# Delta rule and block inverses: small matmuls of different parts of the array written in turns, and both halves of the heads in shared tiles

## The chip, the cores and the metric

One core of a Trainium2 chip runs the whole kernel. The metric is the device time of one execution in microseconds; lower is better. Three runs of the kernel before gave a median of 1875.55 us (1871.42 to 1876.63).

## What is computed

Two layers of a decoder trunk on 1024 tokens of width 1024: an RWKV-7 mixer (16 heads of 64), then differential attention, each followed by a gated per-layer embedding, and a last norm. The change lies in the mixer's recurrence, which the reference writes token by token:

```
def step(state, inp):
    r_t, w_t, k_t, v_t, kk_t, b_t = inp
    sa = jnp.einsum('bhij,bhj->bhi', state, kk_t)
    state = (state * w_t[:, :, None, :] - sa[..., None] * b_t[:, :, None, :]
             + v_t[..., None] * k_t[:, :, None, :])
    y_t = jnp.einsum('bhij,bhj->bhi', state, r_t)
    return state, y_t
```

The kernel works in 16 chunks of 64 tokens. In a chunk the delta rule becomes the product with the inverse of a triangular 64x64 matrix for each head; the state passes from chunk to chunk.

## The kernel before

The 16 heads are two halves, `st` = 0 and 1, of eight heads each: four pairs `p_`, and in a pair the heads `h` = 0 and 1, one on partitions 0 to 63 and one on 64 to 127. A 64x64 product of one head uses 64 rows of the TensorE array (the partitions of its operands) and 64 columns (the partitions of its result). An fp32 product that is written once shows as two matmul records in the trace, each with its own weight load; I call each of them a pass. Transposes and the rounded fp32 products of the dense layers show as one.

**Stage of the inverses** (327 to 598 us). While the dense products for v (`v`, line 75 to 77) and for the gate (`d`) run on PE, four inversions of four chunks each are laid between them. `inv_pb` makes `pb` (line 512; rows of `h`, columns of `st`), which VectorE scales into `nq` (line 514); `inv_diag` inverts 32x32 blocks by 31 steps of two VectorE operations (`tm`, `tb`, lines 541 and 543); `inv_merge` joins the blocks by the products `pg` and `po` (lines 576 and 590; rows and columns of `st`), which ScalarE copies.

**Stage of the chain** (598 to 958 us). For chunk `c`:

- `chain_x`: `xy` gets state times `kkr` (line 827, all rows and columns), then adds `m` times `vu` (line 832; rows of the other half, columns of `st`). ScalarE copies it to `x` (line 842). GpSimd makes `spl`, the decayed state (line 839).
- `chain_u`: `u` is the inverse `ti` times `x` (line 851; rows and columns of `st`); VectorE scales it into the other half of `vu` (line 853).
- `chain_s`: `s` is `kbn` times `vu` (line 867; all rows, columns of `h`), which VectorE adds to `spl` as the new `state` (line 868); the output part of `xy` gets `m` times `vu` (line 871; all rows, the columns of the other half), and ScalarE copies it to `y` (line 874).

Before, each function is called for `st` = 0, then for `st` = 1. Between them `fill` lays other work: `stage1` of the next chunk (`pm`, line 175: 64 rows of `h` and all 128 columns, which VectorE masks into `m` at line 176; the transposes `kbt` at line 168 and `prt` at line 155, read by ScalarE as `kbn` and by VectorE as `bon`) and `d1_pieces` of finished chunks: group norm of `y` (`gst`, lines 904 to 921), its transposes `ytr` (line 932, read by VectorE as `sg`) and the output product `op`. `pm`, `kbt`, `prt` and `ytr` share one ring of two PSUM buffers, the tag that `ps1` holds:

```
pm = ps1[0].tile([P, 4, P], F32, tag=ps1[1], name=f"pm{h}{u}", bufs=2)
```

The order on each engine is fixed when the program is built, by a scheduler that begins with the order in which the program is written, and moves instructions by priority and readiness. At run time each engine takes its instructions in that order.

Of the kernel before, what the change touches and what calls it, by code (L numbers as in the profile page):

```python
# [21 lines left out]
P = 128  # L22
# [4 lines left out]
L = 64  # L27
# [10 lines left out]
def trunk(ctx: ExitStack, tc: tile.TileContext, A, out):  # L38
# [92 lines left out]
    def stage1(st, c):  # L131
# [39 lines left out]
        def mh(h):  # L171
            hs = slice(h * 64, h * 64 + 64)
            pm = ps1[0].tile([P, 4, P], F32, tag=ps1[1], name=f"pm{h}{u}", bufs=2)
            for p_ in range(4):
                T.matmul(pm[:, p_], lhsT=kb[hs, p_], rhs=kkr[hs, p_], start=True, stop=True)  # L175
            V.tensor_tensor(out=m[:, h], in0=pm, in1=early["mmask"][:, st:st + 1].to_broadcast([P, 4, P]), op=ALU.mult)  # L176

        return [(load, 0), (lambda: mh(0), 850), (turn, 430), (lambda: mh(1), 850), (bonus, 430)]

    with NB("ab") as ab, NP("psab") as pp:  # L180
# [313 lines left out]
        def inv_pb(q):  # L494
# [3 lines left out]
            for cc in range(4):  # L498
# [3 lines left out]
                for t, src in ((bb, kb_d), (kk, kkr_d)):  # L502
                    for st in range(2):
                        js = slice(4 * st, 4 * st + 4)
                        nc.sync.dma_start(out=t[:, js], in_=src[js, :, c, st].rearrange("j p l -> p j l"))
                for h in range(2):
                    hs_ = slice(h * 64, h * 64 + 64)
                    pb = pp.tile([P, 4, L], F32, tag="aux", name=f"pb{c}{h}", bufs=2)
                    for st in range(2):
                        o = 64 * st  # L510
                        for p_ in range(4):
                            T.matmul(pb[o:o + 64, p_], lhsT=bb[hs_, 4 * st + p_], rhs=kk[hs_, 4 * st + p_],
                                     start=True, stop=True)
                    V.tensor_tensor(out=nq[:, cc, h], in0=pb,
# [49 lines left out]
        def inv_merge(q):  # L564
# [4 lines left out]
            prhs, pairs = ivt  # L569
            for st in range(2):  # L570
                o = 64 * st
                pg = pp.tile([P, 16, 32], F32, tag="tr", name=f"pg{q}{st}", bufs=2)
                for x in range(16):
                    if x == 8:
                        yield
                    T.matmul(pg[o:o + 64, x], lhsT=pairs[o:o + 64, x], rhs=prhs[o:o + 64, x], start=True, stop=True)
                for y in range(2):
                    r, hs_ = slice(o + 32 * y, o + 32 * y + 32), slice(16 * y, 16 * y + 16)
                    S.copy(pairs[r, :, 32 * y:32 * y + 32], pg[r])
                    S.copy(prhs[r], ti[o + 32:o + 64, hs_, 32:64])  # L580
                yield
            for _ in range(Y2):
# [999 lines left out]
```

## Time and profile before

| | us |
|---|---|
| median of three runs | 1875.55 |
| the profiled execution, its own time | 1872.35 |
| its span, first to last instruction | 1870.6 |
| PE busy | 1786.7 |
| VectorE (DVE) busy | 1348.5 |
| ScalarE (ACT) busy | 762.4 |
| GpSimd (POOL) busy | 635.7 |
| stage of the inverses | 327 to 598 |
| stage of the chain | 598 to 958 |

A busy time counts an engine as busy while any of its instructions is in flight. Matmuls are pipelined, so a PE that is busy throughout can still be waiting for weight loads; what a stream of matmuls costs is read from the distance of one start to the next in the timeline.

### The profile page before, as it was taken

The page shows a single profiled execution, that of the slowest core. Times are in us where ns is not written, and L with a number is a line of the kernel's source. Part 1 is how long each engine was busy: PE and PEld are TensorE (multiplying, and loading weights), DVE is VectorE, ACT ScalarE, POOL GpSimd, SP SyncE. Part 2 cuts the span into 40 slices and gives each one's busy share as a digit, 9 for nine tenths or more (in the row PEclk, how much of TensorE's full clock was granted, in tenths as well). Part 3 has the DMA queues.
Part 4 walks back from the last instruction along what each step waited for, and adds up shares of the span by engine and source line. Part 5 has one row for each costly group of instructions (what it writes and reads, how often), then busy time and mean ns, then how long its engine had stood idle before and what let it go on. Part 6 is the DMA issues. An engine that isn't in the chain of part 4 may idle for free.

```text
span 1870.6 us, 30495 instructions
## 1 busy us (share of the span) xinstructions
PE 1786.7 (96%) x11320; PEld 1485.4 (79%) x11320; DVE 1348.5 (72%) x3083; ACT 762.4 (41%) x1594; POOL 635.7 (34%) x705
## 2 busy tenths in 40 slices
PE   6899899999999999999999999899999999999998
PEld 5677678898787888888878878788888888777786
DVE  7878945587994566666676666877887887866765
ACT  6565533246344222223243433444444444444332
POOL 4436635124224444445420044323323323221200
PEclk9999999898999999999999999999999999999999
DMA  7125344433325443334263321101101101341121
GB/s 260 41 69 161 126 113 96 113 103 102 85 66 178 154 138 102 109 112 124 87 208 113 118 94 48 43 20 52 37 26 52 33 30 52 112 138 33 57 90 68
DMA packets 164402, 175.98 MB, mean 94 GB/s; under 512 B 74845, under 2 KB 127837, under 8 KB 164254
## 3 DMA queue, kind: packets, MB, share of 16 engines
q1 hardware_dynamic: 161950, 169.84, 29.5%
q10 hardware_dynamic: 2304, 4.20, 0.6%
q8 instruction: 89, 1.46, 0.3%
q14 instruction: 59, 0.48, 0.1%
HBM read 124.19 MB, written 49.81 MB: 93 GB/s over the span
## 4 chain that ended last, share of the span: by engine, by line
PE 79%; DVE 14%; issue 2%; DMA 2%; ACT 1%; POOL 0%; SPq 0%; DVEq 0%; ACTq 0%; POOLq 0%
PE qkv L75 6%; PE qkv L76 6%; PE qkv L77 6%; PE d L75 4%; PE d L77 4%; PE d L76 4%; PE pm L175 4%; PE av L1306 3%; DVE xmt L216 2%; PE sc L1266 2%; PE xy L832 2%; PE sc L1267 2%; PE xy L827 2%; PE u L851 2%; PE fg L77 2%
## 5 line engine op out<-in xcount | busy, mean ns | idle before, releaser
L1276 ACT ACTIVATE e<-sc,mx 128x256 f32<-128x256 f32 (+7 forms) x128 | 94.1, 739 | 111.0 <-DVE mx L1273 60.0
L1220 POOL TENSOR_TENSOR rp<-rp,rq 128x128 f32<-128x128 f32 x64 | 34.8, 544 | 239.3 <-DVE rq L1215 191.4
L176 DVE TENSOR_TENSOR m<-pm,mmask 128x512 f32<-128x512 f32 x64 | 44.2, 690 | 67.2 <-PE pm L175 66.4
L1306 PE MATMUL av<-vh,aT 128*128 128x128 f32 x576 | 81.0, 280 | 6.3 <-DVE aT L1302 6.3
L1306 PEld LDWEIGHTS av<-vh,aT 128*128 128x128 f32 x576 | 75.4, 195 | 12.9 <-DVE aT L1302 9.0
L175 PE MATMUL pm<-kkr,kb 64*128 64x128 f32 x512 | 75.8, 286 | 0.0
L1272 DVE TENSOR_REDUCE mxs<-sc 128x1 f32<-128x128 f32 (+6 forms) x112 | 74.1, 681 | 0.5
L1266 PE MATMUL sc<-k,q 128*128 128x512 f32 (+2 forms) x192 | 71.5, 379 | 2.2 <-ACT e L1276 2.2
L175 PEld LDWEIGHTS pm<-kkr,kb 64*128 64x128 f32 x512 | 62.2, 187 | 12.1 <-issue 5.3
L216 DVE SCALAR_TENSOR_TENSOR xmt<-hT,cB,xmt 128x512 f32<-128x512 f32 x64 | 63.8, 1016 | 5.4 <-POOL ti L562 4.9
L164 POOL TENSOR_TENSOR kbp<-kb,plast 128x512 f32<-128x512 f32 x32 | 37.2, 1164 | 87.0 <-PE kbt L168 76.1
L1267 PE MATMUL sc<-k,q 128*128 128x512 f32 (+2 forms) x192 | 64.8, 348 | 0.0
L1308 ACT ACTIVATE o<-av,r 128x128 f32<-128x128 f32 x64 | 23.5, 368 | 90.8 <-PE av L1306 90.8
L1288 DVE SCALAR_TENSOR_TENSOR e<-e,r,e 128x128 f32<-128x128 f32 (+3 forms) x64 | 56.5, 883 | 1.2
L541 DVE TENSOR_TENSOR tm<-tb,nb 128x31 f32<-128x31 f32 (+15 forms) x124 | 53.7, 433 | 3.6
L839 POOL TENSOR_TENSOR spl<-state,plast 64x256 f32<-64x256 f32 x60 | 46.1, 769 | 29.6 <-DVE state L868 21.7
L1214 DVE TENSOR_TENSOR rp<-qkv,rc 128x256 f32<-128x256 f32 x64 | 27.0, 423 | 39.9 <-PE qkv L77 33.0
L543 DVE TENSOR_TENSOR tb<-tb,tm 128x31 f32<-128x31 f32 (+15 forms) x124 | 53.4, 430 | 3.4
L1248 POOL CAST q<-q 64x128 fp32r<-64x128 f32 x128 | 38.8, 304 | 48.8 <-PE sc L1267 44.6
L1239 POOL CAST k<-k 64x256 fp32r<-64x256 f32 x64 | 26.4, 413 | 81.2 <-ACT k L1237 80.0
L1302 DVE COPY aT<-at 128x512 f32<-128x512 f32 (+2 forms) x96 | 52.0, 550 | 1.1 <-PE at L1300 0.4
L1300 PE MATMUL at<-ident,e 128*128 128x128 f32 x288 | 47.4, 277 | 2.9 <-DVE e L1288 2.3
(1180 smaller groups left out, 6155.1 us busy)
## 6 DMA issues: line engine op xcount, KB each, us to landing
pp_d<-ppo SPq DMA_DIRECT2D x32, 256.0 KB, 2.2
kb_d<-kb SPq DMA_DIRECT2D x16, 512.0 KB, 2.6
kkr<-kkr_d SPq DMA_DIRECT2D x32, 256.0 KB, 3.0
kb<-kb_d SPq DMA_DIRECT2D x32, 256.0 KB, 2.9
x<-in_x SPq DMA_DIRECT2D x8, 512.0 KB, 5.3
kkr_d<-ep SPq DMA_DIRECT2D x16, 256.0 KB, 2.6
kkr_d<-rt SPq DMA_DIRECT2D x16, 256.0 KB, 2.6
bb<-kb_d SPq DMA_DIRECT2D x32, 128.0 KB, 2.6
```

The costliest lines, as they stand in the source:

```text
L75: T.matmul(ps, lhsT=ah, rhs=bh, start=start, stop=False)
L76: T.matmul(ps, lhsT=ah, rhs=bl, start=False, stop=False)
L77: T.matmul(ps, lhsT=al, rhs=bh, start=False, stop=stop)
L175: T.matmul(pm[:, p_], lhsT=kb[hs, p_], rhs=kkr[hs, p_], start=True, stop=True)
L216: V.scalar_tensor_tensor(out=t, in0=hT[:, kt, half(hf)], scalar=cB[:, g, kt:kt + 1], in1=t, op0=ALU.mult, op1=ALU.add)
L541: V.tensor_tensor(out=tv, in0=tb[:, j:j + 1, 0:w].to_broadcast([P, n, w]), in1=nb[:, j + 1:32, j:j + 1].to_broadcast([P, n, w]), op=ALU.mult)
L1266: T.matmul(ps[:, b0:b1], lhsT=q1[:, m, ts_], rhs=k1[:, m, b0:b1], start=True, stop=False)
L1267: T.matmul(ps[:, b0:b1], lhsT=q0[i % 2][:, m], rhs=k2[:, b0:b1], start=False, stop=True)
L1272: V.tensor_reduce(out=seed, in_=ps[:, 0:n - P], axis=AX.X, op=ALU.min)
L1276: S.activation(e[:, 0:n], ps[:, 0:n], AF.Exp, scale=-1.0, bias=mx, accum_out=l_[:, m:m + 1])
L1288: V.scalar_tensor_tensor(out=es[0][:, 0:n], in0=es[1][:, 0:n], scalar=r[:, 1:2], in1=es[0][:, 0:n], op0=ALU.mult, op1=ALU.add)
L1306: T.matmul(po, lhsT=aT[kb // 4][:, kb % 4], rhs=c["vh"][:, kb], start=(kb == 0), stop=(kb == i))
```

## The change

`turns` gives each matmul of a list an order dependency on the one before it, without a semaphore: it fixes the order on PE and adds no wait. With it

- `pm` is made for both `h` at once, the two row halves in turns, into both buffers of the ring;
- `pb` is made for both `h` and both `st` in turns (four quarters of the array);
- `pg` and `po` for both `st` in turns, and the copies follow after one more step of the tick;
- the chain's functions take both halves: `xy` (second part), `u` and the output part with `st` = 1 and 0 in turns, `s` with the two `h` in turns. Its matmuls have high priority;
- `vu` and `x` are one tile for both halves, and `vu` of the next chunk is loaded at the head of `chain_x`;
- the two transposes `ytr` of a pair of chunks are called one chunk earlier, at the end of that chunk's list (`ahead`).

No product and no VectorE, ScalarE or GpSimd operation of the mathematics is added or taken away. The core of the diff:

```diff
+    def turns(ms):
+
+        for a, b in zip(ms, ms[1:]):
+            tc.add_manual_dep(b.ins, a.ins.name,
+                              mybir.DependencyInfo(mybir.DependencyClass.NoSync, mybir.DependencyReason.DATA),
+                              reason="turns")
...
-        def mh(h):
-            hs = slice(h * 64, h * 64 + 64)
-            pm = ps1[0].tile([P, 4, P], F32, tag=ps1[1], name=f"pm{h}{u}", bufs=2)
+        def mh():
+
+            pm = [ps1[0].tile([P, 4, P], F32, tag=ps1[1], name=f"pm{h}{u}", bufs=2) for h in range(2)]
+            ms = []
             for p_ in range(4):
-                T.matmul(pm[:, p_], lhsT=kb[hs, p_], rhs=kkr[hs, p_], start=True, stop=True)
-            V.tensor_tensor(out=m[:, h], in0=pm, in1=early["mmask"][:, st:st + 1].to_broadcast([P, 4, P]), op=ALU.mult)
-
-        return [(load, 0), (lambda: mh(0), 850), (turn, 430), (lambda: mh(1), 850), (bonus, 430)]
+                for h in (1, 0):
+                    hs = slice(h * 64, h * 64 + 64)
+                    ms.append(T.matmul(pm[h][:, p_], lhsT=kb[hs, p_], rhs=kkr[hs, p_], start=True, stop=True))
+            turns(ms)
+            for h in range(2):
+                V.tensor_tensor(out=m[:, h], in0=pm[h],
+                                in1=early["mmask"][:, st:st + 1].to_broadcast([P, 4, P]), op=ALU.mult)
+
+        return [(load, 0), (turn, 430), (mh, 850), (bonus, 430)]
...
+                pb = [pp.tile([P, 4, L], F32, tag="aux", name=f"pb{c}{h}", bufs=2) for h in range(2)]
+                ms = []
+                for p_ in range(4):
+                    for st in (1, 0):
+                        o = 64 * st
+                        for h in (1, 0):
+                            hs_ = slice(h * 64, h * 64 + 64)
+                            ms.append(T.matmul(pb[h][o:o + 64, p_], lhsT=bb[hs_, 4 * st + p_],
+                                               rhs=kk[hs_, 4 * st + p_], start=True, stop=True))
+                turns(ms)
...
+            def products(nm):
+                pg = [pp.tile([P, 16, 32], F32, tag="tr", name=f"{nm}{q}{st}", bufs=2) for st in range(2)]
+                ms = []
+                for x in range(16):
+                    for st in (1, 0):
+                        r = slice(64 * st, 64 * st + 64)
+                        ms.append(T.matmul(pg[st][r, x], lhsT=pairs[r, x], rhs=prhs[r, x], start=True, stop=True))
+                turns(ms)
+                return pg
...
+        def vload(c):
+            vu = co.tile([P, 2, 4, 2, L], F32, tag="vu", name=f"vu{c}", bufs=2)
+            for st in range(2):
+                nc.sync.dma_start(out=vu[64 - 64 * st:128 - 64 * st, st].rearrange("p j h l -> p (j h l)"),
+                                  in_=v_d[c * L:(c + 1) * L, st * 512:st * 512 + 512])
+            vus[c] = vu
...
+        def chain_x(c):
+
+            px_, ms = [], []
+            vu2 = vus.pop(c)
+            if c + 1 < NCH:
+                vload(c + 1)
...
+                with tc.high_priority():
+                    ms += [T.matmul(px_[st][:, p_].rearrange("p h l -> p (h l)"), lhsT=kkr[:, p_],
+                                    rhs=state[st][:, p_], start=(p_ == 0), stop=False, skip_group_check=True)
+                           for p_ in range(4)]
+            with tc.high_priority():
+                for p_ in range(4):
+                    for h in range(2):
+                        for st in (1, 0):
+                            xs_, ys_, vu, px = ctx_c[st]
+                            m = units[st, c][2]
+                            ms.append(T.matmul(px[xs_, p_, h], lhsT=m[ys_, h, p_, half_(st)], rhs=vu[ys_, p_, h],
+                                               start=False, stop=True, skip_group_check=True))
+            turns(ms)
+            x = co.tile([P, 4, 2, L], F32, tag="x", name=f"x{c}", bufs=1)
...
+        def chain_u(c):
...
+                        for st in (1, 0):
+                            xs_, x = ctx_c[st][0], ctx_c[st][5]
+                            ms.append(T.matmul(pu[st][xs_, p_, h], lhsT=ti[xs_, (c % 4) * 8 + h * 4 + p_],
+                                               rhs=x[xs_, p_, h], start=True, stop=True))
+            turns(ms)
...
+        def chain_s(c):
...
+                        ms += [T.matmul(pS[half_(h), p_], lhsT=kbn[:, p_, half_(h)], rhs=vu[:, p_, h],
+                                        start=True, stop=True) for p_ in range(4) for h in range(2)]
...
+                        for st in (1, 0):
+                            xs_, ys_, vu, px = ctx_c[st][:4]
+                            ms.append(T.matmul(px[ys_, p_, h], lhsT=units[st, c][2][:, h, p_, half_(1 - st)],
+                                               rhs=vu[:, p_, h], start=False, stop=True, skip_group_check=True))
+            turns(ms)
...
+                    if x == 2 and c < NCH - 3:
+
+                        ahead.append((c + 2, pc[:2]))
+                        pc = pc[2:]
```

Three places of the built order show it. **PE, the transposes at the head of chunk 6** (`xy0`, `xy1` are the halves of the chain's tile, `pm01_6` is `h` 0 of half 1 of chunk 6, `ytr10` a transpose for the finished chunks 2 and 3). Before:

```order
L175 MATMUL pm11_6_6809<-kkr1_6_6630,kb1_6_6631 128x128 x4
L867 MATMUL s1_5_6781<-vu1_5_6654,kbn1_5_6405 64x64 x4
L827 MATMUL xy0_6_6853<-state0_5478,kkr0_6_6626 128x128 x4
L155 MATMUL prt1_6_6837<-ident_60,pr1_6_6834 128x128 x2
L832 MATMUL xy0_6_6853<-vu0_6_6851,m0_6_6628 64x64 x8
L175 MATMUL pm00_7_6893<-kkr0_7_6843,kb0_7_6844 128x128 x4
L827 MATMUL xy1_6_6873<-state1_5480,kkr1_6_6630 128x128 x4
L932 MATMUL ytr10_6899<-ident_60,y1_5925 128x128 x4
L832 MATMUL xy1_6_6873<-vu1_6_6871,m1_6_6632 64x64 x8
```

and now:

```order
L855 MATMUL xy1_6_6872<-state1_5480,kkr1_6_6623 128x128 x4
L185 MATMUL pm11_6_6755<-kkr1_6_6623,kb1_6_6624 128x128
L185 MATMUL pm01_6_6754<-kkr1_6_6623,kb1_6_6624 128x128
L185 MATMUL pm11_6_6755<-kkr1_6_6623,kb1_6_6624 128x128
L185 MATMUL pm01_6_6754<-kkr1_6_6623,kb1_6_6624 128x128
L185 MATMUL pm11_6_6755<-kkr1_6_6623,kb1_6_6624 128x128
L185 MATMUL pm01_6_6754<-kkr1_6_6623,kb1_6_6624 128x128
L185 MATMUL pm11_6_6755<-kkr1_6_6623,kb1_6_6624 128x128
L185 MATMUL pm01_6_6754<-kkr1_6_6623,kb1_6_6624 128x128
L981 MATMUL ytr10_6825<-ident_60,y1_5924 128x128 x4
L864 MATMUL xy1_6_6872<-vu6_6627,m1_6_6625 64x64
L864 MATMUL xy0_6_6867<-vu6_6627,m0_6_6621 64x64
```

`pm` alternates between the row halves and fills both buffers of the ring, and `ytr10`, which needs one of them, stands right behind it.

**PE, `xy` and `u` of chunk 4.** Before, one half after the other:

```order
L832 MATMUL xy0_4_6408<-vu0_4_6406,m0_4_6148 64x64 x8
L832 MATMUL xy1_4_6428<-vu1_4_6426,m1_4_6152 64x64 x8
L932 MATMUL ytr00_6454<-ident_60,y0_5488 128x128 x4
L851 MATMUL u0_4_6503<-x0_4_6424,ti1_2685 64x64 x8
L851 MATMUL u1_4_6513<-x1_4_6444,ti1_2685 64x64 x8
L932 MATMUL ytr01_6465<-ident_60,y0_5488 128x128 x4
```

and now (the piece begins with the last three of 16):

```order
L864 MATMUL xy0_4_6426<-vu4_6151,m0_4_6145 64x64
L864 MATMUL xy1_4_6431<-vu4_6151,m1_4_6149 64x64
L864 MATMUL xy0_4_6426<-vu4_6151,m0_4_6145 64x64
L162 MATMUL prt1_4_6398<-ident_60,pr1_4_6395 128x128 x2
L890 MATMUL u1_4_6505<-x4_6452,ti1_2685 64x64
L981 MATMUL ytr01_6403<-ident_60,y0_5487 128x128 x4
L890 MATMUL u0_4_6504<-x4_6452,ti1_2685 64x64
L890 MATMUL u1_4_6505<-x4_6452,ti1_2685 64x64
L890 MATMUL u0_4_6504<-x4_6452,ti1_2685 64x64
L890 MATMUL u1_4_6505<-x4_6452,ti1_2685 64x64
```

Consecutive matmuls now lie in different rows and columns of the array, and both halves of `u` begin only when both halves of `x` are copied.

**VectorE, between the states of chunk 5 and the first `sg` of chunk 6** (`m1_6` are the evictions of `pm11_6` and `pm01_6` above; `gst2` and `y2` the group norm of chunks 4 and 5). Before:

```order
L868 TENSOR_TENSOR state0_5478<-s0_5_6761,spl0_5_6649 64x4x64
L176 TENSOR_TENSOR m1_6_6632<-pm01_6_6745,mmask_5234 128x512
L868 TENSOR_TENSOR state1_5480<-s1_5_6781,spl1_5_6669 64x4x64
L868 TENSOR_TENSOR state0_5478<-s0_5_6761,spl0_5_6649 64x4x64
L904 TENSOR_REDUCE gst2_7057<-y2_6397 128x16
L176 TENSOR_TENSOR m1_6_6632<-pm11_6_6809,mmask_5234 128x512
L868 TENSOR_TENSOR state1_5480<-s1_5_6781,spl1_5_6669 64x4x64
L905 TENSOR_SCALAR gst2_7057<-gst2_7057 128x16
L159 TENSOR_REDUCE bon_76<-prt1_6_6837 64x2x2 x2
L906 TENSOR_TENSOR y2_6397<-y2_6397,gst2_7057 128x1024
L176 TENSOR_TENSOR m0_7_6845<-pm00_7_6893,mmask_5234 128x512
L935 SCALAR_TENSOR_TENSOR sg1_6608<-ytr10_6899,vecs_65,sg1_6608 128x128 x4
```

and now:

```order
L910 TENSOR_TENSOR state0_5478<-s0_5_6785,spl0_5_6657 64x4x64 x2
L910 TENSOR_TENSOR state1_5480<-s1_5_6796,spl1_5_6661 64x4x64 x2
L166 TENSOR_REDUCE bon_76<-prt0_6_6729 64x2x2 x2
L953 TENSOR_REDUCE gst2_7046<-y2_6414 128x16
L954 TENSOR_SCALAR gst2_7046<-gst2_7046 128x16
L955 TENSOR_TENSOR y2_6414<-y2_6414,gst2_7046 128x1024
L963 TENSOR_REDUCE gst2_7046<-ysq2_7050 128x16
L188 TENSOR_TENSOR m1_6_6625<-pm11_6_6755,mmask_5234 128x512
L188 TENSOR_TENSOR m1_6_6625<-pm01_6_6754,mmask_5234 128x512
L68 TENSOR_SCALAR gst2_7046<-gst2_7046 128x16
L984 SCALAR_TENSOR_TENSOR sg1_6601<-ytr10_6825,vecs_65,sg1_6601 128x128 x4
```

The states of both halves are updated together, and both evictions of `pm` now stand behind two reductions (`gst2`) and a subtraction (`y2`) of the group norm, where before one stood between the states and the other behind one reduction.

## Rows read from the trace of the kernel before

**Rows 1.** The page: busy times with shares, and the chain's shares by engine.

```profile
PE 1786.7 (96%) x11320; PEld 1485.4 (79%) x11320; DVE 1348.5 (72%) x3083; ACT 762.4 (41%) x1594; POOL 635.7 (34%) x705
PE 79%; DVE 14%; issue 2%; DMA 2%; ACT 1%; POOL 0%; SPq 0%; DVEq 0%; ACTq 0%; POOLq 0%
```

**Rows 2.** Windows by stage: us, busy by engine (count), PE clock, DMA share, GB/s.

```profile
327.00:598.00 271.00, 260.33 (x2128) 226.18 (x2126) 207.19 (x367) 116.81 (x190) 74.12 (x56) 0.93 0.36 101
598.00:958.00 360.00, 358.56 (x3388) 302.36 (x3389) 228.95 (x447) 96.99 (x150) 168.41 (x167) 0.99 0.41 124
```

**Rows 3.** Waits of PE in the chain's stage: total us, times, longest.

```profile
PE xy L832 <- DMA vu<-v_d: 1.3, 1, 1.3
```

**Rows 4.** Timeline of PE in chunk 8: start us, length us, what, count.

```profile
783.13 1.06 PE L827 MATMUL xy<-state,kkr 128*128 128x128 f32 x8
784.12 1.16 PE L175 MATMUL pm<-kkr,kb 64*128 64x128 f32 x8
785.20 1.90 PE L832 MATMUL xy<-vu,m 64*64 64x64 f32 x32
787.03 1.09 PE L932 MATMUL ytr<-ident,y 128*128 128x128 f32 x8
788.05 1.90 PE L851 MATMUL u<-x,ti 64*64 64x64 f32 x32
```

**Rows 5.** The same timeline, 8 us later: two column halves meet.

```profile
793.14 0.27 PE L871 MATMUL xy<-vu,m 128*64 128x64 f32 x1
793.19 0.22 PE L867 MATMUL s<-vu,kbn 128*64 128x64 f32 x1
793.24 0.22 PE L871 MATMUL xy<-vu,m 128*64 128x64 f32 x1
793.25 0.22 PE L867 MATMUL s<-vu,kbn 128*64 128x64 f32 x1
793.30 0.22 PE L871 MATMUL xy<-vu,m 128*64 128x64 f32 x1
```

**Rows 6.** Windows of chunk 7 and chunk 8, columns as in rows 2.

```profile
762.20:781.90 19.70, 19.70 (x205) 16.52 (x203) 7.94 (x14) 4.64 (x8) 7.89 (x11) 1.00 0.40 128
781.90:806.00 24.10, 24.10 (x226) 20.61 (x226) 19.94 (x45) 5.63 (x9) 13.41 (x13) 1.00 0.33 95
```

**Rows 7.** Groups of VectorE in these chunks: busy us, mean ns, idle before.

```profile
L176 DVE TENSOR_TENSOR m<-pm,mmask 128x512 f32<-128x512 f32 x8 | 5.5, 690 | 9.1 <-PE pm L175 9.0
L868 DVE TENSOR_TENSOR state<-s,spl 64x256 f32<-64x256 f32 x8 | 3.4, 422 | 4.0 <-PE s L867 3.6 <-issue 0.3
L159 DVE TENSOR_REDUCE bon<-prt 64x4 f32<-64x256 f32 x8 | 3.4, 421 | 0.2
L853 DVE TENSOR_TENSOR vu<-u,rn 64x512 f32<-64x512 f32 x4 | 2.7, 685 | 0.9 <-PE u L851 0.9
L904 DVE TENSOR_REDUCE gst<-y 128x16 f32<-128x1024 f32 x1 | 1.2, 1221 | 0.0
L914 DVE TENSOR_REDUCE gst<-ysq 128x16 f32<-128x1024 f32 x1 | 1.2, 1220 | 0.5 <-ACT ysq L908 0.5
```

**Rows 8.** Groups of ScalarE in these chunks.

```profile
L842 ACT COPY x<-xy 64x512 f32<-64x512 f32 x4 | 2.3, 580 | 6.7 <-PE xy L832 6.7
L908 ACT ACTIVATE ysq<-y 128x1024 f32<-128x1024 f32 x1 | 1.1, 1057 | 4.7 <-DVE y L906 4.7
```

**Rows 9.** Timeline of PE in the inverses' stage: products of both kinds.

```profile
450.73 0.96 PE L512 MATMUL pb<-kk,bb 64*64 64x64 f32 x16
...
541.15 3.71 PE L590 MATMUL po<-prhs,pairs 64*64 64x32 f32 x64
```

**Rows 10.** Windows in the inverses' stage, and chunk 4 (687.0 to 714.8).

```profile
350.00:575.00 225.00, 222.95 (x1839) 193.56 (x1838) 191.47 (x343) 101.90 (x166) 64.28 (x44) 0.95 0.34 95
475.00:550.00 75.00, 75.00 (x528) 59.35 (x528) 71.34 (x138) 33.40 (x52) 19.96 (x13) 0.98 0.22 68
687.00:714.80 27.80, 26.46 (x221) 22.56 (x221) 22.24 (x45) 8.84 (x13) 9.56 (x13) 0.88 0.34 97
```

More of the change, by code (lines that the diff above doesn't have):

```diff
@@ L505, in inv_pb @@
                         nc.sync.dma_start(out=t[:, js], in_=src[js, :, c, st].rearrange("j p l -> p j l"))
-                for h in range(2):
[L507 to L514, printed above, removed]
+                pb = [pp.tile([P, 4, L], F32, tag="aux", name=f"pb{c}{h}", bufs=2) for h in range(2)]
[8 more added lines that the diff above has]
+                turns(ms)
+                for h in range(2):
+                    V.tensor_tensor(out=nq[:, cc, h], in0=pb[h],
                                     in1=rn[:, c, h].unsqueeze(2).to_broadcast([P, 4, L]), op=ALU.mult)
@@ new lines, in chain_u @@
+        def chain_u(c):
+            ti = tis[c // 4]
+            pu = [pp.tile([P, 4, 2, L], F32, tag="us", name=f"u{st}_{c}", bufs=2) for st in range(2)]
+            ms = []
+            with tc.high_priority():
+                for p_ in range(4):
+                    for h in range(2):
+                        for st in (1, 0):
[3 more added lines that the diff above has]
+            turns(ms)
+            for st in range(2):
+                xs_, vu = ctx_c[st][0], ctx_c[st][2]
+                V.tensor_tensor(out=vu[xs_], in0=pu[st][xs_],
+                                in1=rn[xs_, c].rearrange("p h j -> p j h").unsqueeze(3).to_broadcast([64, 4, 2, L]),
+                                op=ALU.mult)
@@ new lines, in chain_s @@
+        def chain_s(c):
+            ms = []
+            if c < NCH - 1:
+                for st in range(2):
+                    vu, spl, kbn = ctx_c[st][2], ctx_c[st][4], units[st, c][1]
+                    pS = pp.tile([P, 4, L], F32, tag="us", name=f"s{st}_{c}", bufs=2)
+                    with tc.high_priority():
+                        ms += [T.matmul(pS[half_(h), p_], lhsT=kbn[:, p_, half_(h)], rhs=vu[:, p_, h],
+                                        start=True, stop=True) for p_ in range(4) for h in range(2)]
+                    for h in range(2):
+                        hs = half_(h)
+                        V.tensor_tensor(out=state[st][hs, :, hs], in0=pS[hs], in1=spl[hs], op=ALU.add)
+            with tc.high_priority():
+                for p_ in range(4):
+                    for h in range(2):
+                        for st in (1, 0):
[3 more added lines that the diff above has]
+            turns(ms)
@@ L974, in weave @@
             return o
-        for st in range(2):
-            vus[st] = vload(st, 0)
+        vload(0)
         later = [[] for _ in range(NCH + 6)]
@@ L1004, in early_row @@
             return lambda: wg.append(gate_row(0, q, None, EG[q], er[0][:, q], False))
+        ahead = []
         EG = (G, G)
@@ L1011, in trunk @@
                 D1[c // 2] = {"y": dt_("y", f"y{c // 2}", 3)}
+            for at_, pc in ahead:
+                if at_ == c:
+                    later[c].extend(pc)
             work = weave(stage1(0, c + 1) + stage1(1, c + 1) if c + 1 < NCH else [], later[c])
```

108 lines of the change are left out of this document (32 added, 76 removed).

## The prediction, made before the changed kernel ran

> **What bounds the kernel now.** I read the page first: PE is busy 96% of the span, and 79% of the chain that ended last runs on it [rows 1]. The windows by stage say where the change can act: in the chain's stage (598 to 958 us) PE is busy for 358.56 of 360 us and VectorE for 228.95, in the inverses' stage for 260.33 of 271 and 207.19 [rows 2]. In the chain PE waits for another engine in a way that matters only once, 1.3 us for the load of `vu` [rows 3]. So PE's own stream sets the time of the chain, and what is saved there is saved, until something else is late.
>
> What a pass costs is read from starts in the timeline of chunk 8. 32 passes of `xy` take 1.83 us from 785.20 to the next group at 787.03, 57 ns each; 32 of `u` look the same; eight of `pm` take 1.08 us (784.12 to 785.20), 135 ns each, the change of tile shape included [rows 4]. These neighbours use the same part of the array. Eight microseconds later, where the program happens to pass from `s` to the output part of `xy`, passes of the two column halves start two by two: 793.14, 793.19, 793.24, 793.25, 793.30 [rows 5]. Each half keeps its own distance of 53 to 58 ns and both run at once. This is what `turns` makes the rule.
>
> **A rule against it.** Both groups of rows 5 use all 128 rows, on different columns, and run side by side [rows 5]. The Trainium skill (TensorE: Matmul & The Clock Gate, Part 3: Packing small matmuls) says that a weight load overlaps matmuls in flight only when the row group differs. The trace disagrees for column halves. By the rule `s` and the output part would gain nothing, and the sum would be 1819.
>
> **The chain, part by part**, for chunks 7 and 8, which take 19.70 and 24.10 us, 43.8 together [rows 6]:
>
> - `pm`: eight groups of eight passes, 8 x 1.08 = 8.7 us. Now four groups of 16, eight on each row half; if the halves run side by side a group takes what eight take now, 1.08 us: 4.3 us less. No row shows two row halves over the same columns side by side. The ends are nothing (they run one after the other) and the full 4.3; a loss is excluded, as the same passes remain and their groups get fewer. I take the full gain, since the nearest row, two column halves, shows no cost of company [rows 5].
> - `xy` (second part) and `u`: 1.83 us each and chunk [rows 4]. Now 16 passes on each half, at 57 ns, and some 0.15 us for the change of tile shape (an estimate: at the 53 ns of rows 5, 32 passes would take 1.70 of the 1.83): 1.07 us. Less 0.76 four times: 3.0 us.
> - `s` and the output part: 64 passes a chunk in halves, 32 x 0.057 + 0.15 = 2.0 us. In chunk 8 they now take about 3.1, as some already run in pairs [rows 5]: less 1.1 twice, 2.2 us.
>
> Together 9.5 us of PE per two chunks, 43.8 to 34.3; eight times 76 us. The first part of `xy` fills the array and stays.
>
> **What is late next.** Until now one half's matmuls covered ScalarE and VectorE of the other. Now both halves hand over together, and three waits appear, as I read the built order.
>
> First, `ytr10` stands right behind `pm` of the next chunk, which fills both buffers of the ring. It must wait for the first eviction `m`, and on VectorE that stands behind four state updates (1.7 us), two `bon` (0.8), a reduction (1.2), a subtraction of the same size (1.2), ScalarE's square (1.06), the next reduction (1.2), and takes 0.7 [rows 7, 8]: 7.8 us, with hand-offs and one small operation 8.4 after the end of `s`. PE comes there earlier: output part 1.1, `prt` and `kbt` 0.9 (six transposes; eight take 1.02), first part of `xy` 2.0 (twice the 0.99 from 783.13 to 784.12), `pm` 1.1, in all 5.1 [rows 4]. So PE stands some 3.3 us in every second chunk. Behind it on PE wait the second part of `xy`, so `x`, `u` and the chain.
>
> Second, `u` waits for two copies to `x`, 2 x 0.58 [rows 8], and `s` for two scalings, 2 x 0.69 [rows 7]. About two thirds of these lie under `kbt` and `pm`, which stand between; I leave 1.0 us per two chunks, more where no dense product stands there.
>
> VectorE as a whole has 27.9 us of work in these two chunks [rows 6], below the new 34.3 + 4.3 = 38.6, so it does not become the bound over two chunks, only inside the heavy one. GpSimd's 21.3 is further away [rows 6].
>
> Waits: 4.3 us for each of six pairs of chunks, 1 us for the first two, which have no transposes to wait for: 28 us. Against it, the load of `vu` a chunk ahead takes away the wait of rows 3 and the lower granted clock behind it: chunk 4 takes 27.80 us at a mean clock of 0.88, chunk 8 with the same work 24.10 at 1.00 [rows 6, 10]: 3 us. The two loads per chunk stay two on SP's queue, issued earlier; their buffer is free one chunk before. `turns` itself carries no semaphore and costs nothing; if the fixed order makes a ready matmul stand behind one that is not, that is within the waits. The chain: 76 + 3 - 28 = 51 us less.
>
> **The inverses.** `pg` and `po` are eight groups of 64 passes, 3.6 us each [rows 9]; two halves side by side halve them: 8 x 1.75 = 14 us. `pb` is 32 groups of 16 passes, 0.96 us with its tail [rows 9], about 1 us with the change of shape, now 16 groups of 32 at two abreast, about 1.1: 32 x 1.0 less 16 x 1.1, 14 us. I assume two and not four abreast for the four quarters, as no row shows more. Together 28 us on PE, 30 with the group changes. But VectorE is close there: 191.5 us busy of 225 between 350 and 575, and 71.3 of 75 (95%) between 475 and 550 [rows 10]; its 31 steps per inverse have to be done before `pg`. At 95% throughout, 191.5 us of work need 201.6: the stage can give up 23 us. I take 23; the ends are 0 and 30.
>
> **The sum.** 51 + 23 = 74 us off the profiled execution's own 1872.35 is 1798; that execution was 3.2 us below the median of 1875.55, so I forecast **1801 us**. Ahead of 327 and behind about 970 us nothing is moved.
>
> **The rivals.**
>
> - *All of it arrives* (the waits fall into work that I did not see): 76 + 3 + 30 = 109 us, 1766. For it: before, PE waited for nothing. Against: the order puts `ytr10` behind a full ring. 0.14.
> - *Row halves do not pair*: `pm` gives nothing, 8 x 4.3 = 34 us more on PE, about half of which fills the new waits: 1818. No row speaks for or against. 0.15.
> - *Only tiles of different rows pair*: `s` and the output part, which use all rows, keep 57 ns a pass, 8 x 2.2 = 18 us more, 1819. Against it stand rows 5. 0.03. This is what the rule of the Trainium skill quoted above comes to here.
> - *The waits are twice as long* (VectorE's list in the heavy chunk holds PE at the second `ytr` and at `s` as well, and the inverses give 10): the chain 76 + 3 - 56 = 23, 33 in all, 1842. For it: VectorE is busy for 19.94 us of chunk 8 [rows 6], and PE's new heavy chunk is hardly longer. 0.14.
> - *The change does not do what it says*: in turns the array takes them one by one. Then only fewer group changes stand against the new waits: about 1871, on either side of no change. Rows 5 speak against it. 0.04.
> - *Slower*: the light chunks now hold small matmuls and waits only, and the granted clock falls to its lower level (1.2 GHz) there, as it did behind the wait in chunk 4, where the mean fell to 0.88 [rows 10]. Work at half the clock takes twice as long; to lose the 74 us, 74 us of PE work in the chain must run so, a quarter of it: it decides once the chain's mean clock is below about 0.8, against 0.99 now [rows 2]. At 0.77 it would be about 1893. For it: one wait of 1.3 us was enough [rows 3, 10]. Against: my waits lie between stretches twice as dense as now. 0.04.
>
> **How the numbers follow.** The forecast has 0.46. 0.3% (5.6 us) is about what can be told from no change; only the case without pairs lies near it. Faster by more: 0.46 + 0.14 + 0.15 + 0.03 + 0.14 and a part of the case without pairs, 0.93; within: 0.03; slower: 0.04. The range runs from 1757, below the case in which all arrives, to 1838, which takes in row halves that do not pair and the shorter part of the long waits; it leaves out 0.17: half the long waits, the two last cases and a little at the lower end.
>
> **What would show it.** In the timeline after, `xy`, `u`, `s` and `pm` start two by two, a group of 32 `xy` passes takes 1.1 us and 16 of `pm` 1.1. PE has new idle time before `ytr`, `u` and `s`, released by VectorE and ScalarE, in sum near 28 us, and the two-chunk period is near 38 us. Wrong I am if `pm` keeps 2 us for 16 passes, if the period is below 36 or above 41, or if the chain's clock falls.

## The result, and the profile after

The changed kernel takes 1828.97 us (median of four runs, 1827.76 to 1830.94) where the kernel before took 1873.49 beside it: a ratio of 0.9763, 95% interval 0.9742 to 0.9785. It is faster by 44.5 us. The forecast was 1801, 74 us below the 1875.55 known then; 1829 lies inside the range (1757 to 1838). The profiled execution has a span of 1826.5 us, and its own time is 1828.3 us.

The page of the kernel after, busy times and the chain that ended last by engine:

```profile
PE 1684.7 (92%) x11320; PEld 1397.6 (77%) x11320; DVE 1350.9 (74%) x3083; ACT 760.4 (42%) x1594; POOL 634.5 (35%) x705
PE 51%; DVE 10%; ACT 2%; issue 1%; DMA 0%; POOL 0%; ACTq 0%; DVEq 0%
```

PE has lost 102 us of busy time against [rows 1], and the kernel only 44. The shares of the chain add up to 64% only, since it is followed back no further than to 656 us; so its 51% for PE can't be set against the 79% of [rows 1]. From chunk 4 to the end of chunk 15 the two can be compared: PE had 91% of the stretch before (687 to 957 us) and has 59% after (667 to 910), VectorE had 1% and has 24%. The windows by stage, from the first `pb` to the first `xy`, from there to the last output part of `xy`, and VectorE's part of the inverses (us, busy by engine with counts, PE clock, DMA share, GB/s):

```profile
325.87:588.20 262.33, 228.43 (x2126) 197.37 (x2126) 210.27 (x368) 117.55 (x192) 81.79 (x58) 0.90 0.39 114
588.20:910.00 321.80, 283.69 (x3377) 239.13 (x3376) 225.76 (x442) 93.05 (x146) 158.67 (x164) 0.94 0.42 130
350.00:556.00 206.00, 186.87 (x1732) 161.64 (x1732) 187.18 (x339) 93.60 (x153) 64.53 (x43) 0.93 0.32 93
```

The same two stretches lasted 270.8 (327.6 to 598.4) and 359.0 us (598.4 to 957.4) before: 8.5 us came from the inverses and 37 from the chain; the rest of the program gave back some 2. In the chain PE now stands idle for 38 us, against 1.4 before [rows 2], and its mean clock is 0.94 instead of 0.99.

The passes do run side by side. Timeline of PE, one `pb` group and chunk 6 (start, length, what, count; idle time before and what ended it in brackets):

```profile
325.87 0.69 PE L527 MATMUL pb<-kk,bb 64*64 64x64 f32 x32
...
704.54 2.05 PE L855 MATMUL xy<-state,kkr 128*128 128x128 f32 x16
706.52 1.16 PE L185 MATMUL pm<-kkr,kb 64*128 64x128 f32 x16
711.72 0.82 PE L981 MATMUL ytr<-ident,y 128*128 128x128 f32 x4 [4.04 <-DVE m L188]
712.47 1.98 PE L864 MATMUL xy<-vu,m 64*64 64x64 f32 x32
...
725.26 1.15 PE L906 MATMUL s<-vu,kbn 128*64 128x64 f32 x32
726.25 1.10 PE L916 MATMUL xy<-vu,m 128*64 128x64 f32 x32
```

16 passes of `pm` take 1.16 us, as long as eight did [rows 4]: row halves pair. 32 of `s` take 1.15. Only the second part of `xy` still takes 1.98, and the windows around it say why:

```profile
706.00:712.00 6.00, 1.96 (x25) 1.65 (x24) 4.72 (x6) 1.06 (x1) 3.86 (x4) 1.00 0.51 150
712.00:715.50 3.50, 3.50 (x42) 3.06 (x41) 2.30 (x10) 1.63 (x3) 0.30 (x1) 0.51 0.00 0
```

PE stood for 4 us, and the next 3.5 us ran at about half the full clock, 1.2 of 2.4 GHz. What PE waits for, 588 to 925 us (total, times, longest; the 6.1 us of `prt` lie at the end of the inverses):

```profile
PE ytr L981 <- DVE m L188: 16.8, 6, 4.1
PE prt L162 <- POOL pr L158: 7.8, 2, 6.1
PE s L906 <- DVE vu L895: 5.3, 6, 3.7
PE xy L855 <- ACT y L923: 5.2, 1, 5.2
PE prt L162 <- DVE m L188: 2.6, 3, 0.9
PE u L890 <- ACT x L878: 2.2, 8, 0.3
```

And VectorE ahead of that wait of `ytr` in chunk 6: the masking of `pm`, which would free the t ring, starts at 710.97, though `pm` is done at 707.7. It stands behind the group norm, whose second reduction itself waits for ScalarE's square:

```profile
705.55 1.22 DVE L953 TENSOR_REDUCE gst<-y 128x16 f32<-128x1024 f32 x1
706.80 0.48 DVE L954 TENSOR_SCALAR gst<-gst 128x16 f32<-128x16 f32 x1
707.31 1.23 DVE L955 TENSOR_TENSOR y<-y,gst 128x1024 f32<-128x1024 f32 x1
709.72 1.22 DVE L963 TENSOR_REDUCE gst<-ysq 128x16 f32<-128x1024 f32 x1 [1.18 <-ACT ysq L957]
710.97 1.29 DVE L188 TENSOR_TENSOR m<-pm,mmask 128x512 f32<-128x512 f32 x2
```

**An account of the chain.** From the starts in the timeline I work out what each pass costs PE: the time to the next start, idle time left out, halved where the granted clock was at its lower level. Before: 352.6 us of work, 1.3 idle, 5.1 lost to the clock. After: 264.5 of work, 37.9 idle, 19.3 lost to the clock. So PE's work fell by 88 us, of which 36.6 came back as idle time and 14.2 as clock. By kind, with half the time at the lower clock taken out: `pm` 66.9 to 41.4, `s` 28.8 to 14.6, `u` 30.5 to 20.7, the second and the output part of `xy` 61.5 to some 33. The account is an estimate: how the edges of the stretches at the lower clock are counted moves the idle time and the clock after by 1 to 2 us each.

### The profile page after: what moved, and what is told of

Same layout as the page of the kernel before. It is cut to its first block, busy times and chain, and to the rows that moved or that the text cites. A ratio compares the mean times of both kernels' runs of the same rounds, so it can differ in the third digit from the quotient of the medians.

```text
span 1826.5 us, 30473 instructions
## 1 busy us (share of the span) xinstructions
PE 1684.7 (92%) x11320; PEld 1397.6 (77%) x11320; DVE 1350.9 (74%) x3083; ACT 760.4 (42%) x1594; POOL 634.5 (35%) x705
## 4 chain that ended last, share of the span: by engine, by line
PE 51%; DVE 10%; ACT 2%; issue 1%; DMA 0%; POOL 0%; ACTq 0%; DVEq 0%
PE qkv L75 6%; PE qkv L76 6%; PE qkv L77 6%; PE av L1359 3%; PE sc L1319 2%; PE sc L1320 2%; PE fg L75 2%; PE fg L76 2%; PE fg L77 2%; PE op L75 2%; PE op L77 2%; PE op L76 2%; PE do L75 1%; PE pg L76 1%; PE pg L77 1%; PE do L76 1%
## 5 line engine op out<-in xcount | busy, mean ns | idle before, releaser
L1359 PEld LDWEIGHTS av<-vh,aT 128*128 128x128 f32 x576 | 75.6, 195 | 12.8 <-DVE aT L1355 8.9
L875 POOL TENSOR_TENSOR spl<-state,plast 64x256 f32<-64x256 f32 x60 | 41.4, 690 | 49.6 <-DVE state L910 42.7
L185 PE MATMUL pm<-kkr,kb 64*128 64x128 f32 x512 | 50.8, 307 | 3.1 <-ACT kbn L176 2.2
L185 PEld LDWEIGHTS pm<-kkr,kb 64*128 64x128 f32 x512 | 40.4, 203 | 12.9 <-issue 6.0
L923 ACT COPY y<-xy 64x512 f32<-64x512 f32 x32 | 18.6, 580 | 71.4 <-PE xy L916 71.0
```

Of the source, the lines that this page charges most:

```text
L185: ms.append(T.matmul(pm[h][:, p_], lhsT=kb[hs, p_], rhs=kkr[hs, p_], start=True, stop=True))
L1359: T.matmul(po, lhsT=aT[kb // 4][:, kb % 4], rhs=c["vh"][:, kb], start=(kb == 0), stop=(kb == i))
```

## Experiments

The theory: pairing works in full, and what is missing was given back where PE stands behind work that nobody waits for, on in-order engines, and in the lower clock that follows each longer stand. The rivals: the gain is not from the turns at all; the wait only moves; PE in the inverses is held by something other than VectorE. The runs come from several chips, on which the kernel before took 1869.3 to 1873.5; a difference of a few microseconds between runs of different chips is one of medians and no more.

**The old order inside the lists** (`serial`), everything else as changed:

```
-            for p_ in range(4):
-                for h in (1, 0):
+            for h in (1, 0):
+                for p_ in range(4):
                     ms.append(T.matmul(pm[h][:, p_], ...))
...
```

> The changed kernel with its lists of small passes in the old order, one part of the array after the other (pb, pg, po, pm, both parts of xy, u, s); the shared tiles, the load of vu a chunk ahead and the order of the pieces stay as changed. Theory (all of the gain is passes that run side by side): the 118 us of PE work that the two traces differ by come back and the waits of 62 us go with them, so about the time before, 1873, between 1860 and 1885; pm of eight passes a part again takes some 2 us for 16. Rival (shared tiles, the early load or the order of pieces carry much of the gain): below 1855.

1862.18 us, ratio to before 0.9951 (0.9919 to 0.9983). The window of its chain, and from its timeline of PE a group of `u` and a border between `s` and the output part:

```profile
596.60:942.10 345.50, 337.03 (x3378) 289.93 (x3376) 232.11 (x445) 98.54 (x152) 156.56 (x165) 0.98 0.43 134
```

```profile
806.10 1.90 PE L890 MATMUL u<-x,ti 64*64 64x64 f32 x32
...
810.52 0.27 PE L916 MATMUL xy<-vu,m 128*64 128x64 f32 x1
810.58 0.22 PE L906 MATMUL s<-vu,kbn 128*64 128x64 f32 x1
810.63 0.22 PE L916 MATMUL xy<-vu,m 128*64 128x64 f32 x1
```

The turns alone carry 33 of the 44 us: without them `u` takes 1.90 us again, as in [rows 4], and most of the new idle time and the clock loss are gone with the gain (by the account 8.5 and 5.3 us are left). About 7 us of the gain stay. By the account PE's work in this chain is 332 us, 21 less than before. 9 of these lie in `s` (19.5 us instead of 28.8): at each border between two parts some passes of the next part already run beside the last of the one before. That the rest comes from longer lists of one shape, which change the tile shape less often, fits, but no run shows it by itself.

**Each stage alone.** `inv_only` puts the turns of `pb`, `pg` and `po` into the kernel before; `chain_only` puts the old inverses into the changed kernel.

> The kernel before with the turns of pb, pg and po alone. Theory (VectorE limits the inverses, so that of 33 us that PE saves there 23 come back as waits for nq, prhs): 10 us faster than before, 1861 to 1867, and the chain as long as before (360 us). Rival (my forecast's 23 us come when the chain is unchanged, the loss being one of the hand-over between the stages): 1850.

> The changed kernel with the inverses of the kernel before. Theory (the two stages add up): 31 to 34 us faster than before, 1837 to 1845, the chain some 329 us. Rival (what the inverses leave over, late tiles or a lowered clock, costs the chain in the changed kernel): the chain below 320 us, 1830 or less.

`inv_only`: 1872.44 us, ratio 1.000 (0.997 to 1.003), no gain. `chain_only`: 1851.55, ratio 0.9881 (0.9834 to 0.9929), 18 us. Together they give 18, and the whole change 44: they don't add up. The windows of the two stages of `chain_only`, those of `inv_only`, and what PE waits for in the chain of `inv_only`:

```profile
327.50:603.80 276.30, 261.10 (x2126) 226.21 (x2126) 210.79 (x368) 118.64 (x192) 79.72 (x58) 0.91 0.38 108
603.80:934.20 330.40, 284.36 (x3376) 239.65 (x3376) 225.00 (x442) 93.33 (x146) 159.76 (x164) 0.93 0.42 127
```

```profile
327.80:585.10 257.30, 231.10 (x2126) 199.45 (x2126) 206.63 (x367) 115.93 (x190) 74.48 (x56) 0.90 0.37 107
585.10:956.90 371.80, 367.24 (x3384) 309.17 (x3384) 226.56 (x442) 95.79 (x149) 161.28 (x166) 0.96 0.39 118
```

```profile
PE xy L847 <- DMA vu<-v_d: 3.1, 2, 2.4
```

The inverses gave 13.5 us and the chain lost 12.8: it waits for the load of `vu`, and its clock is 0.96 instead of 0.99 (8.8 us by the account above). Neither of my readings had this. So the next two runs load `vu` a chunk ahead, without and with the turns of the inverses.

```
-            vu = vus.pop(st, None) or vload(st, c)
+            vu = vus.pop((st, c))
+            if c + 1 < NCH:
+                vus[st, c + 1] = vload(st, c + 1)
...
```

> The kernel before with the load of vu issued a chunk ahead (four buffers; the two x tiles, on different rows, share one to make room). My forecast gave this 3 us (one wait of 1.3 us and the lowered clock behind it in chunk 4). Theory: the wait for vu is gone in every execution, and the time falls by 3 to 8 us, to 1862 to 1867, with less scatter from run to run, since the runs of before differ by 22 us from lowest to highest. Rival (the early load moves nothing): 1869 with the same scatter.

> The same early load of vu, with the turns of pb, pg and po too. Theory (the 13.5 us that the inverses gave when changed alone were lost in the chain to waits for vu and the lowered clock behind them): 10 to 14 us less than with the early load alone, 1850 to 1856. Rival (the chain loses them whatever vu does, for instance to the clock at its start): the same as with the early load alone within 4 us.

`vu_only`: 1874.67, ratio 1.0038 (1.0018 to 1.0057); `inv_vu`: 1858.25, ratio 0.9941 (0.9922 to 0.9960), 16 us less than `vu_only`. The early load is worth nothing by itself, against my 3 us: its chain is 357.2 us against 359.0, but the kernel as a whole is, if anything, 5 us slower, and the part of the program behind the chain took 4 us more in that profile, for a reason that I did not find. But with it the gain of the inverses arrives. The stages of `inv_vu`:

```profile
327.80:585.00 257.20, 230.94 (x2126) 199.34 (x2126) 206.65 (x367) 115.75 (x190) 74.77 (x56) 0.90 0.38 108
585.00:943.20 358.20, 358.20 (x3384) 301.64 (x3384) 225.38 (x441) 95.43 (x149) 162.64 (x166) 0.99 0.40 122
```

That is how the parts of the change belong together: shorter inverses show only where the chain doesn't wait for `vu`. The 16 us of `inv_vu` and the 18 of `chain_only` make 34 of the 44. Of the rest the windows of `chain_only` show two parts. Its inverses, though unchanged, last 276.3 us instead of 270.8, so the moved pieces cost some 5 us at the end of that stage; with the old pieces the changed inverses take 257.3 (`inv_only`) instead of 262.3. And its chain is 9 us longer than that of the whole change, with longer waits (`ytr` 21.0 us instead of 16.8, `xy` for `y` 7.2 instead of 5.2), for a reason that stays open.

**The norm behind the evictions** (`evict_dep`):

```
+                first = V.tensor_reduce(...)
+                for ev in evicts.get(2 * i + 2, []):
+                    turns([ev, first])
...
```

> The changed kernel, with the first reduction of each group norm held behind the four evictions of pm of the next chunk on VectorE (an order without a semaphore). Theory (ytr waits for the t ring because these evictions stand behind the norm's reduction and subtraction): the six waits of ytr, 16.8 us, fall to about 1 us each, and with them most of the half-clock stretches behind them (1.7 us each): 1808 to 1818. Rival (the wait only moves to the next late step, the handover x, u, s or y): 1825 to 1831. Other rival (the norm, now later, delays what follows): slower than 1831.

1824.06 us, ratio 0.9733 (0.9682 to 0.9783): about 5 us less than the changed kernel, not 11 to 20. The waits of its chain:

```profile
PE prt L163 <- DVE m L189: 8.5, 7, 3.3
...
PE ytr L985 <- DVE m L189: 4.7, 6, 0.8
```

The waits of `ytr` went as the theory says, 16.8 to 4.7. But part came back at once at `prt`, which comes next in the same ring: 2.6 us to 8.5. In chunks 5 to 11 this kernel is 8.4 us faster (132.6 us against 141.0); in chunks 0 to 4, where the first norm was held back with no `ytr` to help, it is 5.6 us slower (`best1` below, which leaves the first norm alone, is not: 99.6 us there against 100.5); in chunks 12 to 15 it is 4.4 us longer, but 20 more passes of `op` lie in them, some 4.6 us of work that stood behind the chain.

**The gate rows behind y of chunk 11** (`gate_after`), and both together, the first norm left alone (`best1`). Around the end of chunk 11 of the changed kernel ScalarE shows this:

```profile
824.68 1.15 ACT L718 ACTIVATE pwg0raw<-pwg0raw,vecs 128x1024 f32<-128x1024 f32 x1 [5.17 <-DMA pwg0raw<-in_pwg]
...
829.07 1.18 ACT L923 COPY y<-xy 64x512 f32<-64x512 f32 x2
```

```
+            a = S.activation(r, r, AF.Copy, scale=scale)
+            if 11 in ycopies and nm[:4] == "pwg0":
+                turns([ycopies[11], a])
...
```

> The changed kernel, with the two early gate rows' activations (pwg0raw) held behind the two copies y of chunk 11 on ScalarE. Theory (ScalarE stands 5.2 us in a wait for the load of pwg0raw while the copies y stand behind it, and PE stands for xy and then runs at half clock for some 7 us): 6 to 9 us less than the changed kernel, 1820 to 1823, and no wait of the first part of xy for y. Rival (PE would then stand in the same place for something else): 1827 to 1831.

> The same, and the group norms from the second on held behind the evictions of pm of the next chunk (with the first norm, where no ytr waits, left where it was). Theory (the gains add; holding back the first norm too had cost 5.6 us in the first five chunks and the others had given 8 to 11): 1808 to 1815. Rival (the norms held back are what cost there, so that only the gate rows' gain is left): 1818 to 1823.

`gate_after`: 1834.08, ratio 0.9813 (0.9781 to 0.9845), not faster than the changed kernel, rather slower. The wait of `xy` for `y` is gone and chunk 11 is 5.3 us shorter; but the last three chunks and the stretch behind them take it back, with a new wait of 4.7 us (`ptr` for `n`, 1.3 before). `best1`: 1814.18, ratio 0.9717 (0.9675 to 0.9759): 15 us faster than the changed kernel by the medians, 9 to 11 by the ratios to the kernels before; no run of the one lies among those of the other. The window of its chain, with the same 20 more passes of `op`, and the same place as above in the timeline of PE:

```profile
589.30:900.40 311.10, 283.85 (x3398) 235.63 (x3396) 223.93 (x451) 92.53 (x146) 154.48 (x164) 0.97 0.46 140
```

```profile
705.97 1.16 PE L186 MATMUL pm<-kkr,kb 64*128 64x128 f32 x16
707.91 0.66 PE L988 MATMUL ytr<-ident,y 128*128 128x128 f32 x4 [0.78 <-DVE m L189]
708.51 1.15 PE L868 MATMUL xy<-vu,m 64*64 64x64 f32 x32
```

PE stands 0.78 us, and `xy` behind it runs at full clock. `best1` differs from `evict_dep` in the first norm as well as in the gate rows; the norms from the second on alone were not run, so how the 15 us divide stays open.

**The yardstick, VectorE in the inverses, one half of pm at a time, and two more places** ran on one chip, where the kernel before took 1870.18.

> The changed kernel once more, as the measure for the runs beside it on the same chip: 1824 to 1834, as before. If it lies at 1834 or above, holding back the gate rows alone did no harm; if at 1829 or below, it cost some 5 us.

`after_again`: 1829.37 us, ratio 0.9778 (0.9734 to 0.9821). So holding back the gate rows alone, beside a kernel before of 1869.67, cost some 5 us by the medians; the intervals of the two ratios overlap.

`inv_light` leaves out every second of the steps that invert the diagonal blocks:

```
-                V.tensor_tensor(out=tv, ...)
-                V.tensor_tensor(out=tb[:, j + 1:32, 0:w], ...)
+                if j % 2 == 0:
+                    V.tensor_tensor(out=tv, ...)
+                    V.tensor_tensor(out=tb[:, j + 1:32, 0:w], ...)
```

> The changed kernel with every second of the 31 steps of each of the four inverses left out (60 of 124 pairs of VectorE operations, some 52 us of VectorE's work; the inverses are then others). Theory (VectorE's list holds PE in the inverses: 34 us idle, a lowered clock worth 20): the stage from the first pb to the first xy falls from 262 us to 240 to 250, PE's idle time there to 10 to 20 us. Rival (PE stands there for loads, ScalarE and GpSimd, not for VectorE): 258 to 262 as now.

1823.01 us. Its stage, 328.0 to 575.1:

```profile
328.00:575.10 247.10, 227.27 (x2146) 194.21 (x2145) 164.46 (x250) 112.82 (x187) 75.21 (x55) 0.93 0.36 101
```

PE's busy time is the changed kernel's, 227 against 228, and the stage is 15 us shorter. The waits for what VectorE's list makes (`pb` for `nq` 5.6 us, and `po` and `pg` 10.2 for `prhs`, ScalarE's copies of it, in the changed kernel) are down to 2.8. VectorE's list does hold PE there. Only 6 of the 15 us reach the end, as the chain takes 6 more at a clock of 0.92.

`mh_single` undoes `pm`:

```
...
-        return [(load, 0), (turn, 430), (mh, 850), (bonus, 430)]
+        return [(load, 0), (lambda: mh(0), 850), (turn, 430), (lambda: mh(1), 850), (bonus, 430)]
```

> The changed kernel with pm as before: one head half at a time, a group of eight passes in one buffer, and the old order of the pieces of a unit. Theory (side by side, pm saves PE some 25 us, and its hold on both buffers of the t ring gives back about as much in waits of ytr and the clock behind them): within 8 us of the changed kernel, and the waits of ytr below 3 us in all. Rival (the waits are those of the handover, whatever pm does): 20 us or more slower than the changed kernel.

1820.57 us (1817.94 to 1823.28), ratio 0.9730 (0.9677 to 0.9782): 9 us faster than the changed kernel beside it. The windows of its two stages, the main wait of PE in its chain, and two `pm` groups in the timeline:

```profile
327.80:584.30 256.50, 229.78 (x2125) 199.06 (x2125) 206.40 (x367) 115.68 (x190) 74.62 (x56) 0.91 0.38 108
584.30:904.80 320.50, 305.74 (x3378) 258.40 (x3376) 229.57 (x448) 96.44 (x148) 160.96 (x166) 0.95 0.45 137
```

```profile
PE xy L858 <- DVE m L183: 7.4, 11, 3.6
```

```profile
722.73 1.16 PE L182 MATMUL pm<-kkr,kb 64*128 64x128 f32 x8
...
727.17 1.16 PE L182 MATMUL pm<-kkr,kb 64*128 64x128 f32 x8
```

By the account above `pm` costs PE 65.0 us here and 41.4 in the changed kernel, 24 more; idle time in the chain is 14.7 instead of 37.9, and the clock loss 15.1 instead of 19.3. No wait of `ytr` is left. So pairing `pm` gave PE 24 us and took back 27. Without it the chain is 1.3 us shorter, the stretch from there to the last `op` 3.3, and the inverses 5.8, where PE's wait for GpSimd's `pr` is down to 2.6 us. The theory holds, and beyond what it said: this part of the change was a loss. `pm` and the order of the pieces went back together here, so their shares stay open.

One stand accounts for much of what this kernel still loses. In chunk 10 an eviction of `pm` again stands behind the norm:

```profile
783.56 1.76 PE L858 MATMUL xy<-vu,m 64*64 64x64 f32 x28 [3.56 <-DVE m L183]
```

```profile
783.00:796.60 13.60, 13.04 (x89) 10.93 (x90) 8.93 (x26) 3.01 (x5) 2.76 (x3) 0.50 0.14 40
```

PE stands 3.6 us, the next 13.6 us run at half the clock, and the chunk takes 31.3 us where chunks 4, 6 and 8 take 21.0.

`best2` clears two more places. The first, on GpSimd, at the end of the inverses of the changed kernel: `pr` is cut in two by a split that nobody waits for, and PE stands 6.12 us for it (timelines of GpSimd and of PE).

```profile
580.75 2.34 POOL L72 TENSOR_TENSOR wpl<-wp,wph 128x1024 fp32r<-128x1024 f32 x1
583.05 1.70 POOL L157 TENSOR_TENSOR pr<-kkr,kb 128x256 f32<-128x256 f32 x1
584.72 2.34 POOL L72 TENSOR_TENSOR wpl<-wp,wph 128x1024 fp32r<-128x1024 f32 x1
587.03 0.60 POOL L158 TENSOR_TENSOR pr<-pr,vecs 128x256 f32<-128x256 f32 x1
```

```profile
587.68 0.69 PE L162 MATMUL prt<-ident,pr 128*128 128x128 f32 x2 [6.12 <-POOL pr L158]
```

```
-                split(h, lo, r, V if nm == "p" else G)
+                split(h, lo, r, V if nm == "p" else G, prs.get((1, 0), ()) if nm == "wp" else ())
...
-            split(h, lo, r, V)
+            split(h, lo, r, V, scaled[2] if kt == 2 else ())
```

> The fastest so far (norms held behind the evictions, gate rows behind y of chunk 11), and two more places where work that nobody waits for stands ahead on an in-order engine: GpSimd's two splits wpl held behind the second pr of chunk 0 (PE stands 6 to 7 us for its prt at the start of the chain), VectorE's split rwo2l behind the scalings vu of chunk 2 (s stands 3.7 us). Theory (both waits go, and the lowered clock behind them): 8 to 14 us less than 1814, 1800 to 1806. Rival (PE then stands for the next late step, as after the gate rows alone): 1810 to 1815.

1814.99 us (1812.97 to 1816.34), ratio 0.9699 (0.9656 to 0.9742): the same as `best1`. Both waits have shrunk (`prt` for `pr` 8.4 to 2.3 us, `s` for `vu` 5.7 to 2.3), and the inverses are 3.5 us shorter. But the chain is 4.1 us longer: its first chunk takes 23.2 us instead of 19.0. The rival was right: PE stood in other places, for instance 3.4 us at `kbt` for GpSimd's `kbp`.

`best1` and `best2` are the fastest measured, 14 us below the changed kernel. `pm` one half at a time with the norms and gate rows held back was not tried.

## Why the prediction was right, and where it was not

**Pairing: right.** 32 passes of `xy` or `u` take 1.15 us (forecast 1.1), 16 of `pm` 1.16 (1.1), `s` with the output part 2.0 from 725.26 to 727.28 (2.0). PE's work in the chain fell by 88 us where I had 76. That the paired products come so near to the 76, at some 78, is luck: two sizes were wrong and cancel. `pm` gave 25 and not 34, since its passes are often cut in two groups by others (2 and 14 at 719.67 and 720.51). `s` and the output part gave some 27 and not 18: I took the 3.1 us of chunk 8 for every chunk, where chunk 7 takes 4.4 and the mean is 3.7. The other 10 us lie in products that the turns do not touch (the first part of `xy`, `op` and `pps`), which cost less a pass than before, as some of them do in `serial`; 2 of them are eight passes of `op` that moved behind the chain. The rival in which row halves do not pair falls, and so does the one in which only tiles of different rows do. The Trainium skill (TensorE: Matmul & The Clock Gate, Part 3: Packing small matmuls) says that a weight load overlaps matmuls in flight only when the row group differs. The trace disagrees: `s` uses all rows in both of its halves, and its 32 passes, each with its own weight load, take 1.15 us in turns, where 32 of `u`, of the same length, take 1.90 in the old order.

**The wait of `ytr`: right in cause and size.** Forecast 3.3 us in each heavy chunk, behind the norm on VectorE; measured 16.8 in six, 4.1 at most, and `evict_dep` brings them down to 4.7 by the order on VectorE alone. The handovers were smaller than the forecast's 8 us: `u` 2.2, `s` 1.6 without the one stand named next.

**Not seen: three single stands**, 15 us together: `prt` behind GpSimd's `wpl` (6.1), `xy` behind ScalarE's gate rows (5.2), `s` behind the split `rwo2l` on VectorE (3.7). The first lies at the end of the inverses, where PE stood 2.9 us for `pr` before as well; the others, and some 7 us of small waits (`prt`, the output part of `xy`, `op`), are why the chain has 36.6 us of new idle time where I had 28.

**The step that failed is the clock.** The 3 us for the early load of `vu` and "the lower granted clock behind" its wait were the only term that I gave it, a gain; the rival on the clock I took for a matter of all or nothing below 0.8. Measured: the chain's clock falls from 0.99 to 0.94, one of the signs that I had named for being wrong (the other two did not come: 16 passes of `pm` take 1.16 us, and two chunks take 40.2 us on average, inside 36 to 41), and costs some 14 us more than before. Nor did `vu_only` show the 3 us. Most of the stretches at the lower clock begin in or right behind a stand of PE, as at 712.0: 14.2 us of clock on 36.6 us of idle time, so that a wait costs some 40% more than its own length on average. Single ones differ widely: 4 us of idle time at 708 brought 3.5 us at half the clock, 3.6 us in `mh_single` brought 13.6, and 0.78 in `best1` none. With the clock, the chain's sum is 88 less 36.6 less 14.2, 37 where I had 51.

**The inverses: the mechanism right, the size wrong.** I let VectorE run at 95% throughout: 23 us. It ran at 91% (187.18 of 206), and its last inverse was done (its transpose starts) 223 us after the first `pb` (548.88) instead of 238 (565.47): 15 us. 6 of these were lost at the end of the stage: the stand for `pr` grew from the 2.9 us before (line below) to 6.1, PE newly stands 1.9 for `kbn`, and from 575 us on its clock is 0.52, where it was 1.00 before. The moved pieces, with `pm` in turns, caused this, as `inv_only`, `mh_single` and `chain_only` show, so that 8.5 came through. `pb` ran four abreast and not two; it saved PE 14.7 us by the account (28.6 to 13.9), about what I had, as did `pg` and `po` (14.5, forecast 14); but PE's own gain was not the limit: `inv_light` shows VectorE's list to be that.

```profile
PE prt L155 <- POOL pr L151: 2.9, 1, 2.9
```

**The sum.** 30 us are missing: 14.5 in the inverses, 17 of clock and 9 of waits in the chain, 2 elsewhere, less 12 that PE's work gave more. That the time lies inside the range owes something to luck: without these 12 it would have been some 1841, above the 1838 at its end.

## What to carry to other kernels

Part of the work saved on the engine that sets the pace comes back as waits at rings and queues that had been covered by it (here 36.6 of 88 us); before pairing, count for each ring how many buffers the paired step holds at once, and who wants one next. Price every new wait with what the clock takes behind it, and look on each in-order engine for work that nobody waits for ahead of work that PE waits for. Taking away one such stand alone gave between 5 us less and 5 us more here, by the medians; two together, with the first norm left alone, gave 15.

## What the runs showed that I had not expected

- Four quarters of the array run four abreast: 32 passes of `pb` take 0.69 us, with starts 7 ns apart inside a round and rounds 58 ns apart, where 16 took 0.96 [rows 9].
- Without any turns, passes of the next part begin beside the last ones of the part before: in `serial`, `s` and the output part start in turn from 810.52 to 810.75, though the built order has all of `s` first. So what the section on the kernel before says of each engine taking its instructions in the built order does not hold to the pass on PE.
- Shorter inverses alone gave nothing (ratio 1.000), and the early load of `vu` alone gave nothing (1.0038, rather slower), but both together 11 us (0.9941).
- Pairing `pm`, with the order of pieces that goes with it, takes a third off its time on PE (65.0 to 41.4 us) and yet makes the kernel 9 us slower.
